# Compressed-attention values with their high, low and high parts stacked in 96 rows, one matmul per head in place of three

## The chip, the cores and the metric

The kernel runs on one core of a Trainium2 chip. The metric is the device time of one execution in microseconds (us), lower is better. Matmul operands are float32 numbers split in two `fp32r` parts, a high part (what the conversion keeps) and a low part (what it loses), so that a product needs three matmuls: high by high, high by low, low by high. The helper `mm3` issues these three, on lines 171, 172 and 173.

## The reference

One layer of a decoder trunk on 512 tokens of width 2048: RMS norm, an input projection, eight forgetting-attention heads (FoX) and eight NSA query heads in two key/value groups, an output projection, and a SwiGLU feed-forward part of width 5632. An NSA head adds three branches, each with a sigmoid gate. The change touches the compressed branch alone, in which 31 compressed keys and values per group stand for the 512 tokens:

```python
k_cmp = _rms_norm(_compress(kc.reshape(B, T, G, Dh), cmp_pos_k, cmp_w_k), cmp_k_norm)
v_cmp = _compress(vc.reshape(B, T, G, Dh), cmp_pos_v, cmp_w_v)
...
s_c = jnp.einsum("bqgrd,bngd->bgrqn", qn_b, k_cmp).astype(f32) * scale
s_c = s_c - slopes[None, :, :, None, None] * dist_c
p_c = _masked_softmax(s_c, dist_c >= 0)
o_c = jnp.einsum("bgrqn,bngd->bqgrd", p_c.astype(dt), v_cmp)
...
o_nsa = g_b[..., 0:1] * o_c + g_b[..., 1:2] * o_s + g_b[..., 2:3] * o_w
```

## The kernel before

The core works through stages: a first pass over the sixteen k tiles of the input (`x`), which makes the first projections (`ps_first`, lines 651 to 683) and the row sum of squares (`acc`, then `fr_r1` and `ps_r1`, lines 259 and 260); the remaining projections, woven by `weave` with the attention heads; the output projection; and the feed-forward part, which begins at about 750 us of the span.

In the attention stage the generator `nsa(h)` is the side work and the projections of coming heads are the main work; `weave` hands out steps of both. Instructions then go through a scheduler of the programming layer, which may reorder them on each engine by its own estimates, except where `pin` keeps them. Each engine executes its own queue in order.

The compressed values of both groups are made once in `compress("vc")`: 32 matmuls accumulate `z`, its parts `zs` are multiplied by `rows` (a matrix of ones that adds a row of `z` to the positional term), and the result `zr`, 64 rows (32 for each group), is split by `split` into `Vc[:, 0]` (high, a ScalarE copy, line 82) and `Vc[:, 1]` (low, a VectorE subtraction, line 79). Keys (`"kc"`) go through the same lines.

`compressed(h, q, o)` makes a head in three steps. First the scores, softmax and gate; the probabilities go to columns `gs` of a 64-column tile `pc[g]`, whose other 32 columns stay zero from a memset on line 286. Then four transposes (line 539) put the probabilities of the four token blocks into a PSUM tile of 64 rows, `pcT`, of the tag "t" (two buffers), and `split2` makes the two parts `ptc`. Last, `mm3` adds the product with `Vc` to the head's output `o`:

```python
mm3(o, Vc[:, 0], Vc[:, 1], *pt, False, True)
```

All 64 rows take part; the zero columns of `pc[g]` cancel the other group. This is the last product of the head, after the selected branch (`pt_s`) and the window branch (`pt_w`); `keep` then copies `o` (line 449).

Of the kernel before, what the change touches and what calls it, by code (L numbers as in the profile page):

```python
# [9 lines left out]
F32 = mybir.dt.float32  # L10
FR = mybir.dt.float32r
AF = mybir.ActivationFunctionType
OP = mybir.AluOpType
# [4 lines left out]
P = 128  # L18
D = 2048
T = 512  # L20
# [3 lines left out]
NB = T // P  # L24
# [46 lines left out]
def hybrid_layer(ctx: ExitStack, tc: tile.TileContext, xT, vec, ffb, wfg, wfirst, win, cmpw, wout, wgu, wdn, out):  # L71
    nc = tc.nc
# [5 lines left out]
    def tt(*args, op):  # L78
        return pin(nc.vector.tensor_tensor(*args, op=op))  # L79

    def act(*args, **kw):
        return pin(nc.scalar.activation(*args, **kw))  # L82
# [10 lines left out]
    ap_ = att.enter_context(tc.tile_pool(name="att", bufs=1))  # L93
    ps = ctx.enter_context(tc.tile_pool(name="ps", bufs=1, space=PSUM))
# [6 lines left out]
    def big(i):  # L101
        at = i * 2 * T + OFF_BIG[i]
        return bigm[:, at:at + 2 * T].rearrange("p (s t) -> p s t", s=2)
# [23 lines left out]
    def ftile(name):  # L127
        return pers.tile([P, T], F32, tag="f", name=name, bufs=4)

    def split(dst, src, scale=None, neg=None):  # L130

        if scale is None:
            h = act(dst[:, 0], src, AF.Copy)
            tt(dst[:, 1], src, dst[:, 0].bitcast(F32), op=OP.subtract)
            return h
        else:
            nc.scalar.activation(dst[:, 0], src, AF.Copy, scale=scale)
            nc.vector.scalar_tensor_tensor(dst[:, 1], src, scale, dst[:, 0].bitcast(F32),
                                           op0=OP.mult, op1=OP.subtract)
# [4 lines left out]
    def split2(dst, src, scale=None):  # L144

        if scale is None:
            h = act(dst[0], src, AF.Copy)
            tt(dst[1], src, dst[0].bitcast(F32), op=OP.subtract)
        else:
            h = act(dst[0], src, AF.Copy, scale=scale)  # L150
            nc.vector.scalar_tensor_tensor(dst[1], src, scale, dst[0].bitcast(F32), op0=OP.mult, op1=OP.subtract)
        return h
# [17 lines left out]
    def mm3(o, lh, ll, rh, rl, start, stop):  # L170
        nc.tensor.matmul(o, lh, rh, start=start, stop=False)  # L171
        nc.tensor.matmul(o, lh, rl, start=False, stop=False)  # L172
        nc.tensor.matmul(o, ll, rh, start=False, stop=stop)  # L173
# [60 lines left out]
    def v1(i):  # L234
        return vt[:, i:i + 1]

    ident = pers.tile([P, P], F32, name="ident")
# [42 lines left out]
    mc = ap_.tile([P, NB, 32], F32, name="mc")  # L280
    nc.vector.tensor_scalar(mc, dc, 0.0, None, op0=OP.is_ge)
    nc.gpsimd.affine_select(dc, dc, pattern=[[P, NB], [-16, 32]], compare_op=OP.is_ge, fill=FAR, base=-31, channel_multiplier=1)
    pc = []
    for g in range(2):
        t = ap_.tile([P, NB, 64], F32, name=f"pc{g}")
        nc.vector.memset(t, 0.0)
        pc.append(t)

    gains = ap_.tile([P, 6], F32, name="gains")
    nc.vector.tensor_scalar_mul(gains, vt[:, 0:6], -0.5 / HD)  # L290
# [8 lines left out]
    nc.vector.tensor_tensor(rowsf, ident[:, :64], ident[:, 64:], op=OP.add)  # L299
    rows = ap_.tile([P, 64], FR, name="rows")  # L300
    nc.vector.tensor_tensor(rows, rowsf, rowsf[:, 31:32].to_broadcast([P, 64]), op=OP.add)
    rcol = ap_.tile([P, NB], F32, name="rcol")


# [22 lines left out]
    def loose(name, shape=(P, T)):  # L327
        return oxp.tile(list(shape), FR, tag="ox", name=name, bufs=16)
# [148 lines left out]
    def compress(which):  # L477

        z = ps.tile([P, T], F32, tag="s", name=f"z_{which}", bufs=2)[:, :2 * P].rearrange("p (a c) -> p a c", a=2)
        wi = 0 if which == "kc" else 4  # L480
        for b in range(8):
            st = oxp.tile([P, T], F32, tag="ox", name=f"ws_{which}{b}", bufs=16)
            nc.sync.dma_start(st, cmpw[wi + b // 2, :, b % 2 * T:(b % 2 + 1) * T])
            wp = ap_.tile([P, 2, T], FR, tag="kv", name=f"wp_{which}{b}", bufs=5)
            split(wp, st)
            for jj in range(4):
                l = 4 * b + jj
                ws = slice(jj * P, (jj + 1) * P)
                nc.tensor.matmul(z, live[which, l // 16][:, l % 16 * P:(l % 16 + 1) * P], wp[:, :, ws],
                                 start=(l == 0), stop=(l == 31))  # L490
                if l % 2:
                    yield

        zs = ap_.tile([P, 2, 2 * P], FR, tag="nb", name=f"zs_{which}", bufs=2)
        split(zs, z.rearrange("p a c -> p (a c)"))
        yield
        r = ps.tile([P, T], F32, tag="t", name=f"zr_{which}", bufs=2)[:64, :P]
        for hl in range(2):
            nc.tensor.matmul(r, rows, zs[:, hl, :P], start=(hl == 0), stop=False)
            nc.tensor.matmul(r, rows[:64], zs[:64, hl, P:], start=False, stop=(hl == 1))  # L500
        if which == "kc":
            zks = ftile("zks")[:64, :P]
            ss = ap_.tile([64, 4], F32, name="ss")
            nc.scalar.activation(zks, r, AF.Square, accum_out=ss[:, 0:1])
            rsqrt(ss[:, 1:2], ss[:, 0:1], float(HD), ss[:, 2:3])
            nc.vector.tensor_scalar_mul(zks, r, ss[:, 1:2])
            yield
            zkT = ps.tile([P, 64], F32, tag="t", name="zkT", bufs=2)
            nc.tensor.transpose(zkT, zks, ident[:64, :64])
            split(Kc, zkT, v1(V_CK))  # L510
        else:
            split(Vc, r)

    def compressed(h, q, o):
        g = h // 4
        slope = 2.0 ** -(h + 1)
        s = ps.tile([P, NB, 64], F32, tag="m", name=f"sc{h}")
        gs = slice(32 * g, 32 * g + 32)
        for i in range(NB):
            qs = slice(i * P, (i + 1) * P)  # L520
            nc.tensor.matmul(s[:, i, :], q[0][:, qs], Kc[:, :, gs], start=True, stop=False)
            nc.tensor.matmul(s[:, i, 32:64], q[1][:, qs], Kc[:, 0, gs], start=False, stop=True)
        t = ap_.tile([P, NB, 32], F32, tag="ct", name=f"ct{h}", bufs=2)
        st = ap_.tile([P, 3, NB], F32, tag="st", name=f"stc{h}", bufs=4)
        nc.vector.scalar_tensor_tensor(t, dc, slope, s[:, :, 0:32], op0=OP.mult, op1=OP.add)
        nc.vector.tensor_tensor(t, t, s[:, :, 32:64], op=OP.add)
        nc.vector.tensor_reduce(st[:, 0], t, axis=AX.X, op=OP.min)
        nc.vector.tensor_tensor(t, t, st[:, 0, :, None].to_broadcast([P, NB, 32]), op=OP.subtract)
        nc.scalar.activation(t, t, AF.Exp, scale=-1.0)
        nc.vector.tensor_tensor(t, t, mc, op=OP.mult)  # L530
        nc.vector.tensor_reduce(st[:, 1], t, axis=AX.X, op=OP.add)
        nc.vector.tensor_scalar_max(st[:, 2], st[:, 1], 1e-30)
        nc.vector.reciprocal(st[:, 2], st[:, 2])
        nc.vector.tensor_tensor(st[:, 2], st[:, 2], gate[:, :, 3 * h], op=OP.mult)
        nc.vector.tensor_tensor(pc[g][:, :, gs], t, st[:, 2, :, None].to_broadcast([P, NB, 32]), op=OP.mult)
        yield
        b = ps.tile([P, T], F32, tag="t", name=f"pcT{h}", bufs=2)
        for i in range(NB):
            nc.tensor.transpose(b[:64, i * P:(i + 1) * P], pc[g][:, i, :], ident)
        pt = [loose(f"ptc{h}{p}")[:64] for p in range(2)]  # L540
        split2(pt, b[:64])
        yield
        mm3(o, Vc[:, 0], Vc[:, 1], *pt, False, True)
        yield

    qq = ap_.tile([P, 2, 2, T], FR, name="qq")
# [1 line left out]
    cumd = dr.tile([NH, T], F32, name="cumd")  # L548
    ncq = ap_.tile([P, NB, NH], F32, name="ncq")
    Kc = ap_.tile([P, 2, 64], FR, name="Kc")  # L550
    Vc = ap_.tile([64, 2, P], FR, name="Vc")
    tokens = {}

    def gates():
# [101 lines left out]
    for k in range(NK):  # L656
# [4 lines left out]
        t = big(k)  # L661
# [10 lines left out]
        for j in range(4):  # L672
            c = slice(j * P, (j + 1) * P)
            mm3(first[j], wp[:, 0, c], wp[:, 1, c], t[:, 0], t[:, 1], k == 0, k == NK - 1)
        for hl in range(2):
            nc.tensor.matmul(first[4][:64], wf[:, k], t[:, hl], start=(k == 0 and hl == 0),
                             stop=(k == NK - 1 and hl == 1))
# [73 lines left out]
    for i, h in enumerate(order[:-1]):  # L751
        t = big(i)
# [3 lines left out]
    t = big(NK - 1)  # L756
# [48 lines left out]
    for m in range(NK):  # L805
        n = m // 2 + HALF * (m % 2)
# [231 lines left out]
    for j in range(NJ):  # L1038
        for which in range(2):
            q = [ps.tile([P, T], F32, tag=tag, name=f"q{which}{j}_{i}", bufs=BUFS[tag])  # L1040
                 for i, tag in enumerate(SETS[which])]
            for g in range(NG):
                i = (2 * j + which) * NG + g
# [15 lines left out]
                for wp in range(2):  # L1059
                    for kk in range(2):  # L1060
# [3 lines left out]
                        for fa, fb, b, h in PROD:  # L1064
                            o = q[b][:, h * 256:(h + 1) * 256]
                            for xp in range(2 - wp):
                                nc.tensor.matmul(o, w[wp][:, fb, cs], a[:, xp, fa],  # L1067
                                                 start=(k == 0 and h == 0 and wp == 0 and xp == 0),
                                                 stop=(g == NG - 1 and kk == 1 and wp == 1), skip_group_check=True)
# [24 lines left out]
    def banks(name, tags):  # L1094
        return [ps.tile([P, T], F32, tag=tag, name=f"{name}_{i}", bufs=BUFS[tag]) for i, tag in enumerate(tags)]
# [67 lines left out]
    for ps_ in range(4):  # L1163
        p, second = ps_ // 2, ps_ % 2
        b = [banks(f"pd{ps_}{i}", t) for i, t in enumerate(TAGS)]
# [151 lines left out]
```

## Time and profile before

| what | value |
|---|---|
| median of 3 runs | 2114.24 us (2113.95 to 2114.7) |
| profiled execution, its own time | 2114.38 us |
| its span in the trace | 2112.6 us |
| NSA heads' compressed products in the trace | 153 to 403 us of the span |
| feed-forward part | from about 750 us |

Times in the trace count from the start of the span. PE is TensorE, PEld its weight loads, DVE is VectorE, ACT is ScalarE, POOL is GpSimd. A timeline row gives the start, the duration, the engine, the line, the operation with output and inputs, the shape of the part of the array that a matmul or weight load uses (128\*128 is the whole array; the first number is rows), and the tile's shape. Durations of matmuls overlap, since they are pipelined; what one costs in a full queue is read from the distance of two starts. A text in brackets says how long the engine idled before the instruction and what ended the idle time.

### The profile page before, as it was taken

The numbers are of one execution on the slowest core, as the hardware profiler recorded it, in microseconds if no ns is written. First come the engines' busy times: TensorE is split into PE (matmuls) and PEld (weight loads), VectorE is DVE, ScalarE is ACT, GpSimd is POOL, SyncE is SP. The second block draws the span as 40 slices with busy tenths as digits, with TensorE's granted clock in tenths as the row PEclk, the third lists the DMA queues.
The fourth block names the chain that finished last, engine by engine and source line by source line (L and its number), as shares of the span: only waits on it lengthen the run. The fifth ranks groups of instructions, "written<-read, shape, count | busy, mean of one in ns | idle before, by whom it ended". The sixth has DMA issues, their size and how long they took to land.

```text
span 2112.6 us, 37997 instructions
## 1 busy us (share of the span) xinstructions
PE 2101.6 (99%) x15675; PEld 1974.6 (93%) x15675; DVE 1675.4 (79%) x2458; ACT 999.7 (47%) x1242; POOL 190.7 (9%) x283
## 2 busy tenths in 40 slices
PE   9999999999999999999999999999999999999999
PEld 7878988888988888999999999999999999999999
DVE  6667667554567454999999999899999987889898
ACT  5555555444455343544334343343343455565554
POOL 0000000111211000111111111111111000000000
PEclk9999999999999999999999999999999999999999
DMA  5422111222222444676776777777787798579865
GB/s 196 160 75 62 61 58 58 65 86 85 90 85 75 152 137 137 170 188 202 193 195 189 193 197 182 201 187 184 205 191 195 225 335 270 151 233 329 302 174 149
DMA packets 113486, 349.63 MB, mean 165 GB/s; under 512 B 13592, under 2 KB 13592, under 8 KB 113312
## 3 DMA queue, kind: packets, MB, share of 16 engines
q1 hardware_dynamic: 85552, 270.33, 39.5%
q0 software_dynamic: 22144, 52.44, 14.0%
q10 hardware_dynamic: 5616, 24.43, 2.9%
q8 instruction: 122, 2.00, 0.4%
q14 instruction: 52, 0.43, 0.1%
HBM read 318.56 MB, written 74.73 MB: 186 GB/s over the span
## 4 chain that ended last, share of the span: by engine, by line
PE 85%; issue 9%; DVE 3%; POOL 1%; ACT 1%; DMA 0%; POOLq 0%; SPq 0%; ACTq 0%; DVEq 0%
PE q L1067 39%; PE pd L1206 13%; PE pd L1211 6%; PE po L172 3%; PE po L173 3%; PE po L171 3%; PE ps_vs L369 2%; PE ps_vf L369 1%; PE ps_qn L171 1%; PE ps_qn L173 1%; PE ps_qn L172 1%; POOL nbf L628 1%; PE ps_first L171 1%; PE ps_first L173 1%; PE ps_first L172 1%
## 5 line engine op out<-in xcount | busy, mean ns | idle before, releaser
L82 ACT ACTIVATE bigm<-r 128x1792 fp32r<-128x1792 f32 x174 | 298.2, 1714 | 461.1 <-PE q L1067 263.4
L79 DVE TENSOR_TENSOR bigm<-r,bigm 128x1792 fp32r<-128x1792 f32 x174 | 351.5, 2020 | 13.2 <-ACT bigm L82 12.7
L79 DVE TENSOR_TENSOR r<-r 128x512 f32<-128x512 f32 x522 | 267.2, 512 | 27.5 <-DMA r<-wgu 15.2
L1067 PE MATMUL q<-bigm 128*128 128x256 f32 x1848 | 217.5, 276 | 0.2 <-ACT bigm L82 0.2
L1067 PE MATMUL q<-formy,bigm 128*128 128x256 f32 x1848 | 217.1, 276 | 0.0
L1067 PE MATMUL q<-forma,bigm 128*128 128x256 f32 x1848 | 216.8, 276 | 0.0
L1067 PE MATMUL q<-formx,bigm 128*128 128x256 f32 x1848 | 216.8, 276 | 0.0
L1067 PEld LDWEIGHTS q<-bigm 128*128 128x128 f32 x1848 | 213.3, 188 | 0.6 <-ACT bigm L82 0.4
L1067 PEld LDWEIGHTS q<-formy,bigm 128*128 128x128 f32 x1848 | 213.1, 188 | 0.1
L1067 PEld LDWEIGHTS q<-forma,bigm 128*128 128x128 f32 x1848 | 213.0, 188 | 0.1
L1067 PEld LDWEIGHTS q<-formx,bigm 128*128 128x128 f32 x1848 | 212.9, 188 | 0.0
L124 POOL DMA_DIRECT2D wsum<-wdn x176 | 119.8, 687 | 878.7 <-ACT bigm L82 773.7
L1206 PE MATMUL pd<-bigm 128*128 128x256 f32 x1200 | 146.9, 276 | 0.0
L1206 PEld LDWEIGHTS pd<-bigm 128*128 128x128 f32 x1200 | 141.0, 188 | 0.0
L79 DVE TENSOR_TENSOR bigm<-wd,bigm 128x1024 fp32r<-128x1024 f32 (+1 forms) x62 | 107.8, 1739 | 12.3 <-ACT bigm L82 12.2
L82 ACT ACTIVATE bigm<-rawm 128x768 fp32r<-128x768 f32 (+2 forms) x72 | 66.0, 927 | 98.2 <-PE pd L1211 63.8
L369 PE MATMUL ps_vf<-wp_vf,bigm 128*128 128x256 f32 x768 | 101.7, 282 | 0.0
L171 PE MATMUL po<-bigm,wp_o 128*128 128x512 f32 x256 | 99.7, 389 | 0.0
L172 PE MATMUL po<-bigm,wp_o 128*128 128x512 f32 x256 | 99.7, 389 | 0.0
L173 PE MATMUL po<-bigm,wp_o 128*128 128x512 f32 x256 | 99.6, 389 | 0.0
L369 PEld LDWEIGHTS ps_vf<-wp_vf,bigm 128*128 128x128 f32 x768 | 95.1, 189 | 1.5 <-issue 0.7
L82 ACT ACTIVATE bigm<-wd 128x1024 fp32r<-128x1024 f32 (+1 forms) x62 | 91.1, 1469 | 10.7 <-DVE wd L79 6.1
(479 smaller groups left out, 3975.8 us busy)
## 6 DMA issues: line engine op xcount, KB each, us to landing
r<-wgu SPq DMA_DIRECT2D x174, 512.0 KB, 4.3
wsum<-wdn POOLq DMA_DIRECT2D x176, 256.0 KB, 5.1
rawm<-ad SPq DMA_DIRECT2D x44, 512.0 KB, 6.9
wd<-wdn SPq DMA_DIRECT2D x40, 512.0 KB, 6.0
wd<-wsum SPq DMA_DIRECT2D x40, 512.0 KB, 7.0
ad<-cb ACTq DMA_DIRECT2D x22, 896.0 KB, 6.0
rawm<-ad SPq DMA_DIRECT2D x44, 384.0 KB, 3.8
ws_o<-wout SPq DMA_DIRECT2D x28, 512.0 KB, 3.6
```

Of the source, the lines that this page charges most:

```text
L79: return pin(nc.vector.tensor_tensor(*args, op=op))
L82: return pin(nc.scalar.activation(*args, **kw))
L124: d = nc.gpsimd.dma_start(step[0], step[1], **step[2])
L171: nc.tensor.matmul(o, lh, rh, start=start, stop=False)
L172: nc.tensor.matmul(o, lh, rl, start=False, stop=False)
L173: nc.tensor.matmul(o, ll, rh, start=False, stop=stop)
L369: nc.tensor.matmul(z[b][:, t * 2 * HD:(t + 1) * 2 * HD], x[:, xp, at], wp[w][:, ws], start=(c == 0 and kk == 0 and t == 0 and n == 0), sto ...
L628: nc.gpsimd.tensor_scalar(nb[:, :n], ck[:, :n], ncq[:, i, h:h + 1], 1.0, op0=OP.add, op1=OP.mult)
L1067: nc.tensor.matmul(o, w[wp][:, fb, cs], a[:, xp, fa], start=(k == 0 and h == 0 and wp == 0 and xp == 0), stop=(g == NG - 1 and kk == 1 and ...
L1206: nc.tensor.matmul(b[q][k][:, h * 256:(h + 1) * 256], w[0][:, fb, q * P:(q + 1) * P], a[xp][:, fa], start=(j == 0 and h == 0 and xp == 0), ...
L1211: nc.tensor.matmul(b[q][k][:, h * 256:(h + 1) * 256], w[1][:, fb, q * P:(q + 1) * P], a[0][:, fa], start=False, stop=(j == NJ - 1), skip_g ...
```

## The change

Three parts are stacked in the 96 contraction rows of one matmul: values high, low, high against probabilities high, high, low. The rows of only the head's own group are used, so 3 times 32 rows suffice.

- `rows3` is `rows` with each group's 32 columns repeated three times (three VectorE copies at the start). For the values `compress("vc")` multiplies `zs` by `rows3` of each group: eight matmuls instead of four, into 96 rows.
- `Vc` becomes a list of two tiles of 96 rows; each is one copy by ScalarE and one VectorE subtraction on rows 32 to 63.
- `pc` becomes one 96-column tile per head, written by one VectorE multiplication that repeats the probabilities three times; the two memsets go.
- The four transposes give 96 rows; one ScalarE copy makes all high parts and one VectorE subtraction turns rows 64 to 95 into low parts.
- One matmul per head takes the place of `mm3`.

```diff
-    pc = []
-    for g in range(2):
-        t = ap_.tile([P, NB, 64], F32, name=f"pc{g}")
-        nc.vector.memset(t, 0.0)
-        pc.append(t)
...
+    rows3 = ap_.tile([P, 2, 3, 32], FR, name="rows3")
+    for n in range(3):
+        nc.vector.tensor_copy(rows3[:, :, n], rows.bitcast(F32).rearrange("p (g c) -> p g c", g=2))
...
-        r = ps.tile([P, T], F32, tag="t", name=f"zr_{which}", bufs=2)[:64, :P]
-        for hl in range(2):
-            nc.tensor.matmul(r, rows, zs[:, hl, :P], start=(hl == 0), stop=False)
-            nc.tensor.matmul(r, rows[:64], zs[:64, hl, P:], start=False, stop=(hl == 1))
+        r = ps.tile([P, T], F32, tag="t", name=f"zr_{which}", bufs=2)
+        r, by = ([r[:64, :P]], [rows]) if which == "kc" else (
+            [r[:96, g * P:(g + 1) * P] for g in range(2)], [rows3[:, g].rearrange("p n c -> p (n c)") for g in range(2)])
+        for n, (o, m) in enumerate(zip(r, by)):
+            for hl in range(2):
+                nc.tensor.matmul(o, m, zs[:, hl, :P], start=(n == 0 and hl == 0), stop=False, skip_group_check=True)
+                nc.tensor.matmul(o, m[:64], zs[:64, hl, P:], start=False, stop=(hl == 1), skip_group_check=True)
...
-            split(Vc, r)
+            for o, v in zip(r, Vc):
+                nc.scalar.activation(v, o, AF.Copy)
+                nc.vector.tensor_tensor(v[32:64], o[32:64], v[32:64].bitcast(F32), op=OP.subtract)
...
-        nc.vector.tensor_tensor(pc[g][:, :, gs], t, st[:, 2, :, None].to_broadcast([P, NB, 32]), op=OP.mult)
+        pc = ap_.tile([P, NB, 96], F32, name="pc")
+        nc.vector.tensor_tensor(pc.rearrange("p i (n c) -> p n i c", n=3), t[:, None].to_broadcast([P, 3, NB, 32]),
+                                st[:, 2, None, :, None].to_broadcast([P, 3, NB, 32]), op=OP.mult)
         yield
         b = ps.tile([P, T], F32, tag="t", name=f"pcT{h}", bufs=2)
         for i in range(NB):
-            nc.tensor.transpose(b[:64, i * P:(i + 1) * P], pc[g][:, i, :], ident)
-        pt = [loose(f"ptc{h}{p}")[:64] for p in range(2)]
-        split2(pt, b[:64])
-        yield
-        mm3(o, Vc[:, 0], Vc[:, 1], *pt, False, True)
+            nc.tensor.transpose(b[:96, i * P:(i + 1) * P], pc[:, i, :], ident)
+        pt = loose(f"ptc{h}")
+        nc.scalar.activation(pt[:96], b[:96], AF.Copy)
+        nc.vector.tensor_tensor(pt[64:96], b[64:96], pt[64:96].bitcast(F32), op=OP.subtract)
+        yield
+        nc.tensor.matmul(o, Vc[g], pt[:96], start=False, stop=True)
         yield
...
-    Vc = ap_.tile([64, 2, P], FR, name="Vc")
+    Vc = [ap_.tile([96, P], FR, name=f"Vc{g}") for g in range(2)]
```

More of the change, by code (lines that the diff above doesn't have):

```diff
@@ L503, in compress @@
             ss = ap_.tile([64, 4], F32, name="ss")
-            nc.scalar.activation(zks, r, AF.Square, accum_out=ss[:, 0:1])
+            nc.scalar.activation(zks, r[0], AF.Square, accum_out=ss[:, 0:1])
             rsqrt(ss[:, 1:2], ss[:, 0:1], float(HD), ss[:, 2:3])
-            nc.vector.tensor_scalar_mul(zks, r, ss[:, 1:2])
+            nc.vector.tensor_scalar_mul(zks, r[0], ss[:, 1:2])
             yield
```

## The prediction

> **What bounds the kernel now.** I read the page first, for the engine that is never free; then the stretches around the change, to see whether this holds there; then the timeline of TensorE at the product that is changed.
>
> ```profile
> PE 2101.6 (99%) x15675; PEld 1974.6 (93%) x15675; DVE 1675.4 (79%) x2458; ACT 999.7 (47%) x1242; POOL 190.7 (9%) x283
> PE 85%; issue 9%; DVE 3%; POOL 1%; ACT 1%; DMA 0%; POOLq 0%; SPq 0%; ACTq 0%; DVEq 0%
> ```
>
> TensorE is busy for 99% of the span, and the chain that ended last runs over it for 85%. Busy does not mean well used, since pipelined matmuls overlap in their durations: a microsecond is won where starts lie closer together or a start goes away.
>
> ```profile
> core 0: us, PE busy (x) PEld busy (x) DVE busy (x) ACT busy (x) POOL busy (x), PEclk, DMA share, GB/s
> 345.00:403.00 58.00, 57.40 (x395) 51.91 (x394) 39.13 (x111) 29.58 (x67) 3.58 (x4) 1.00 0.18 56
> ```
>
> In this stretch of the attention stage, the last two NSA heads, TensorE idles for 0.60 of 58 us, VectorE works 39.13 us (67%), DMA is at 0.18, and the granted clock is 1.00. So VectorE, ScalarE and DMA have room, and what TensorE loses or gains there is lost or gained by the kernel; later stages take their weights as TensorE consumes them, so they only start earlier.
>
> **The product of a head.** This is the last product of head 0, with the matmuls around it:
>
> ```profile
> 175.35 0.39 PE L173 MATMUL ps_qn<-bigm,wp_qn 128*128 128x512 f32 x1
> 175.67 0.49 PE L171 MATMUL on<-ptc,Vc 64*128 64x512 f32 x1
> 176.00 0.39 PE L172 MATMUL on<-ptc,Vc 64*128 64x512 f32 x1
> 176.23 0.39 PE L173 MATMUL on<-ptc,Vc 64*128 64x512 f32 x1
> 176.56 0.50 PE L171 MATMUL ps_kw<-bigm,wp_kw 128*128 128x512 f32 x1
> 176.90 0.39 PE L172 MATMUL ps_kw<-bigm,wp_kw 128*128 128x512 f32 x1
> ```
>
> ```profile
> 175.67 0.18 PEld L171 LDWEIGHTS on<-ptc,Vc 64*128 64x128 f32 x1 [0.36 <-issue]
> ```
>
> Two matmuls of 512 columns in the same array shape start 0.23 us apart (176.00 to 176.23). Where the shape goes from 128\*128 to 64\*128 the distances are 0.32 and 0.33, and on the way back 0.33 and 0.34; the weight load starts together with its matmul after 0.36 us of "issue". From 175.35 to 176.90 lie five starts in 1.55 us; at 0.23 they would take 1.15. So the two changes of shape cost 0.40 us per head.
>
> ```profile
> L171 PE MATMUL on<-ptc,Vc x8: 492/493/493, 175.7 to 401.7; 64*128 64x512 f32 x8
> ```
>
> The same lengthened first matmul (492 to 493 ns against 0.39 us of the others) stands in all eight heads, so head 0 speaks for all.
>
> In the changed program as built, the one matmul per head carries the shape 128\*128, as 96 rows are more than 64. Then no change of shape is left, and of the five starts two are gone: 3 x 0.23 = 0.69 us. That saves 1.55 - 0.69 = 0.86 us per head, of which 2 x 0.23 = 0.46 is matmuls and 0.40 is shape; 8 x 0.86 = **6.9 us less**. If the shape change stayed, it would be 8 x 0.46 = 3.7.
>
> **The transposes** go from 64 to 96 columns, and from the shape 128\*64 to 128\*128. I compare four of `pcT` with four of `pT_w`, which have the full shape already:
>
> ```profile
> 274.68 0.40 PE L173 MATMUL ps_qn<-bigm,wp_qn 128*128 128x512 f32 x1
> 274.92 0.60 PE L539 MATMUL pcT<-ident,pc 128*64 128x128 f32 x4
> ...
> 275.58 0.39 PE L172 MATMUL ps_qn<-bigm,wp_qn 128*128 128x512 f32 x1
> ```
>
> ```profile
> 163.76 0.39 PE L173 MATMUL ps_qn<-bigm,wp_qn 128*128 128x512 f32 x1
> 163.99 0.60 PE L423 MATMUL pT_w<-ident,p_w 128*128 128x128 f32 x4
> ...
> 164.66 0.39 PE L172 MATMUL ps_qn<-bigm,wp_qn 128*128 128x512 f32 x1
> ```
>
> From the matmul ahead to the second behind it is 0.90 us in both. I take 0 for this edit. The Trainium skill, page TensorEngine Tiling (Array Packing), section Key Properties, says that changing the tiling mode, and not just the tile, drains TensorE; 128x64 is one of the configurations that the page lists. By that sentence the transposes would pay for two changes per head now and the edit would take them away; the trace shows such a price where the number of rows changes and none where only columns do. I go by the rows here, and keep the other as a rival.
>
> **`compress("vc")`** issues four matmuls more, two pairs of a full-height and a 64-row one. The nearest rows are the same pairs of the keys:
>
> ```profile
> 106.29 0.22 PE L499 MATMUL zr_kc<-zs_kc,rows 128*64 128x128 f32 x1
> 106.44 0.27 PE L500 MATMUL zr_kc<-zs_kc,rows 64*64 64x128 f32 x1
> 106.64 0.28 PE L499 MATMUL zr_kc<-zs_kc,rows 128*64 128x128 f32 x1
> 106.85 0.27 PE L500 MATMUL zr_kc<-zs_kc,rows 64*64 64x128 f32 x1
> 107.05 0.51 PE L171 MATMUL ps_kw<-bigm,wp_kw 128*128 128x512 f32 x1
> ```
>
> A pair takes 0.35 (106.29 to 106.64) to 0.41 us (106.64 to 107.05). In the changed order the two new pairs follow the last old one directly, as the second pair here follows the first, so I take 0.41: **0.8 us more**, once, between 0.7 and 0.8. The extra copy and subtraction for `Vc` (both of 128 columns) run on ScalarE and VectorE beside TensorE: 0.
>
> **`rows3`** adds three VectorE copies of 128x64 in the first pass, where VectorE is not idle:
>
> ```profile
> 10.43 0.22 DVE L301 TENSOR_TENSOR rows<-rowsf 128x64 fp32r<-128x64 f32 x1
> 10.57 1.48 DVE L683 TENSOR_TENSOR acc<-acc,sq 128x512 f32<-128x512 f32 x2
> 11.97 0.75 DVE L138 SCALAR_TENSOR_TENSOR bigm<-x,vt,bigm 128x512 fp32r<-128x512 f32 x1
> 12.63 0.68 DVE L683 TENSOR_TENSOR acc<-acc,sq 128x512 f32<-128x512 f32 x1
> 13.23 0.75 DVE L138 SCALAR_TENSOR_TENSOR bigm<-x,vt,bigm 128x512 fp32r<-128x512 f32 x1
> 13.89 0.69 DVE L79 TENSOR_TENSOR w0p<-w,w0p 128x512 fp32r<-128x512 f32 x1
> ```
>
> ```profile
> 14.63 0.30 PEld L173 LDWEIGHTS ps_first<-bigm,w0p 128*128 128x128 f32 x2 [0.21 <-DVE w0p L79]
> 1.26 0.43 DVE L242 CAST ones<-onesf 128x128 fp32r<-128x128 f32 x1
> ```
>
> Each row starts before the one ahead has ended, without a gap, and TensorE waits for the low part of `w0p` that ends this run. The copies stand behind the first `acc`, so their time reaches TensorE in full. From below: the 128x64 `rows` takes 0.14 us to the next start, so 3 x 0.14 = 0.4. From above: 3 x 0.43 of the largest such cast (twice the columns) = 1.3. A gain is excluded, since work is only added here; the two memsets that go stood before 2 us, ahead of the first data. I take **0.5 us more**, nearest to the row of the same size.
>
> The scheduler also moves the first matmul of the row sum (`ps_r`) over a hundred matmuls forward in TensorE's queue, to just behind five `wf` matmuls:
>
> ```profile
> 31.58 0.63 ACT L82 ACTIVATE fr_r<-acc 128x512 fp32r<-128x512 f32 x1 [1.03 <-DVE acc L683]
> 31.95 1.31 PE L676 MATMUL ps_first<-bigm,wf 128*64 128x512 f32 x5
> ```
>
> Its input is there at 32.21, and TensorE gets to it at about 31.95 + 5 x 0.23 = 33.10. Everything behind it in the queue would wait with it, but 0.9 us are left, and the copies delay both sides alike: 0.
>
> **The probabilities.** `pc` is written with 384 elements per partition instead of 128.
>
> ```profile
> L539 PE MATMUL pcT<-ident,pc x32: 270/272/301, 168.3 to 397.7; 128*64 128x128 f32 x32
> L535 DVE TENSOR_TENSOR pc<-ct,stc x8: 280/292/294, 163.8 to 391.2; 128x128 f32<-128x128 f32 x8
> ```
>
> ```profile
> 159.96 0.41 DVE L79 TENSOR_TENSOR pt_s<-pT_s,pt_s 128x256 fp32r<-128x256 f32 x1
> ```
>
> From 0.29 us at 128 elements and 0.41 at 256, 384 take about 0.53: 0.24 more per head. In the first head the transposes start 4.5 us after `pc`, in the last about 6; that covers it. Without cover it would be 8 x 0.24 = 1.9 us. `pc` has a single buffer, but eight heads lie between 168.3 and 397.7, some 33 us apart, so its transposes have long ended.
>
> ```profile
> 209.17 0.68 DVE L79 TENSOR_TENSOR ptc<-pcT,ptc 64x512 fp32r<-64x512 f32 x1
> ```
>
> ```profile
> 211.41 0.49 PE L171 MATMUL on<-ptc,Vc 64*128 64x512 f32 x1
> ```
>
> The one matmul now waits for the low part as well, which before only the second did. In head 1 that part ends at 209.85, 1.56 us ahead of the start. Queued behind the matmul are the next projections, so a late part would stop TensorE; with 0.24 us added it is not late. In the last two heads the scheduler reorders a few steps of VectorE and TensorE; of the 0.60 us of idle time there some may go or as much may come: 0, plus or minus 0.6.
>
> **Sum.** -6.9 + 0.8 + 0.5 = -5.6 us. From the profiled execution's 2114.38 us (1.8 more than its span of 2112.6) this gives 2108.8; the median of the runs lies 0.14 lower, so **2108.6 us**. With the bounds (0.7 to 0.8, 0.4 to 1.3, plus or minus 0.6) the forecast itself lies between 2107.8 and 2110.0.
>
> **The rivals.** A measurement of this kernel can tell about 0.2% from no change, 4.2 us: below 2110.0 is faster, above 2118.5 slower.
>
> *Shape change stays.* If 96 rows are loaded like a partial array, the 0.40 us per head stay: -3.7 + 0.8 + 0.5 = -2.4, 2111.8 us, no change that can be told. For it: the row above shows the price for 64 rows, and no row has 96. Against it: the built program's 128\*128. Chance 0.10.
>
> *Column changes cost too.* If the transposes pay the 0.40 us per head that the row changes pay, 3.2 us more go: 2105.4 us. That is the skill's sentence above taken at its word. Against it stand the two equal 0.90 us. Chance 0.04.
>
> *The low part comes late (slower).* The one matmul has its place behind VectorE's subtraction. It decides from 1.56 us of delay in head 1; were VectorE 3 us late in every head with that slack, TensorE would stand 1.44 us eight times, 11.5 us, and 2108.6 would become 2120.1. For it: VectorE runs 0.53 us per head in one go where it ran 0.29. Against it: 0.24 is far from 1.56, and VectorE is at 67%. Chance 0.04.
>
> **How the numbers follow.** The forecast has 0.82, the rivals 0.10, 0.04 and 0.04. Of the forecast's 0.82 about 0.04 falls above 2110.0. Faster: 0.78 + 0.04 = 0.82. Same: 0.10 + 0.04 = 0.14. Slower: 0.04. The range takes in the forecast's bounds with a microsecond below for gaps that close behind the earlier matmuls, and reaches up to the first rival: 2106.8 to 2112.0.
>
> **What would show it.** In the changed profile: matmuls `on<-ptc` with shape 128\*128, eight of them, the start behind each 0.23 us later and no "issue" ahead; transposes still 0.90 us from matmul to matmul; three copies after 10.5 us and a wait of about 0.7 us on `w0p` at 15 us; two new pairs near 143 us. It would be wrong if `on<-ptc` idled on VectorE, or if 0.32 us starts were left around it.

## The result, and the profile after

| | before | after |
|---|---|---|
| median of 20 runs each, us | 2114.48 (2113.74 to 2115.24) | 2109.94 (2109.4 to 2145.72) |
| ratio, 95% interval | | 0.998 (0.9974 to 0.9986) |
| profiled execution, us | 2114.38 | 2109.57 |
| its span, us | 2112.6 | 2107.9 |

The change makes the kernel faster by 4.5 us, 0.2%; 2108.6 us (-5.6 from the trace) was predicted. The median lies within the stated range of 2106.8 to 2112.0 us, and only 0.06 us below the 2110.0 that the prediction set as the bound of faster. Two slow executions of about 2145 us make the upper end of the runs after and are left out of the ratio; the trace of `e2_one64`, used below, is of such an execution, with the extra time (35.9 us) behind the last product.

The page after, its busy times and the shares of the chain that ended last:

```profile
PE 2096.4 (99%) x15663; PEld 1972.8 (94%) x15663; DVE 1677.6 (80%) x2460; ACT 999.8 (47%) x1243; POOL 190.8 (9%) x283
PE 84%; issue 9%; DVE 3%; ACT 1%; POOL 1%; DMA 0%; POOLq 0%; SPq 0%; ACTq 0%; DVEq 0%
```

The kernel is as bound by TensorE as it was. TensorE's count of matmuls falls by 12: 16 products less, 4 matmuls of `compress("vc")` more. The stretches, with the same columns as before:

```profile
345.00:403.00 58.00, 57.38 (x399) 52.41 (x398) 39.90 (x110) 30.52 (x68) 3.58 (x4) 1.00 0.14 46
```

TensorE still idles for only 0.62 of 58 us and the granted clock is 1.00; it gets through 399 records there where it got through 395. VectorE has 39.90 us for 39.13.

**The product.** TensorE's timeline after, around the product of head 0, and the eight products in one row (duration as minimum/median/maximum in ns, then first and last start):

```profile
176.20 0.39 PE L173 MATMUL ps_qn<-bigm,wp_qn 128*128 128x512 f32 x1
176.43 0.40 PE L552 MATMUL on<-ptc,Vc 96*128 96x512 f32 x1
176.67 0.40 PE L171 MATMUL ps_kw<-bigm,wp_kw 128*128 128x512 f32 x1
176.90 0.40 PE L172 MATMUL ps_kw<-bigm,wp_kw 128*128 128x512 f32 x1
```

```profile
L552 PE MATMUL on<-ptc,Vc x8: 393/395/397, 176.4 to 398.1; 96*128 96x512 f32 x8
```

From the projection matmul ahead to the second one behind, 1.55 us has become 0.70 (176.20 to 176.90). Every start is 0.23 or 0.24 us from the last, and the median product takes 395 ns where the first of three took 493. The profile writes the shape as 96\*128, not 128\*128, and it costs nothing all the same.

**A ledger by segments.** Between one head's product and the next both kernels issue the same matmuls (180, 228, 221, 165, 148, 180 and 212 records for heads 1 to 7), in the same order but for a few ahead of heads 5, 6 and 7. So each segment of the trace can be set beside the other's by its starts: a *product* from the matmul ahead of it to the second behind it, an *interval* from there to the matmul ahead of the next product. This is the one for head 5, whose ends stand in these rows, of before and then of after:

```profile
315.12 0.39 PE L172 MATMUL ps_qn<-bigm,wp_qn 128*128 128x512 f32 x1
...
342.20 0.28 PE L173 MATMUL on<-pt_w,vs 128*128 128x256 f32 x1
```

```profile
311.96 0.40 PE L172 MATMUL ps_qn<-bigm,wp_qn 128*128 128x512 f32 x1
...
339.84 0.29 PE L173 MATMUL on<-pt_w,vs 128*128 128x256 f32 x1
```

It took 27.08 us before and takes 27.88 after: 0.8 us of what the product saves is given back there. The whole ledger, each kernel less before, in us (segments of several kernels that are told of below stand beside it; the times up to 141 us are counted from the span's start):

| segment | after | `e1_shape` | `e3_pc128` | `e4_zrfull` | `h1_nonorm` |
|---|---|---|---|---|---|
| up to the first row sum of `vc` (141 us) | -0.12 | +0.20 | +0.81 | -0.36 | -0.13 |
| row sums of `vc` | +0.98 | +0.01 | +0.99 | -0.16 | +0.98 |
| eight products | -6.75 | -3.07 | -6.78 | -6.76 | -6.76 |
| interval ahead of head 4's product | +0.25 | +0.08 | +0.03 | +0.27 | +0.54 |
| of head 5's | +0.79 | +0.25 | +0.80 | +0.79 | -0.03 |
| of head 7's | +0.57 | +0.42 | +0.56 | +0.54 | +0.21 |
| intervals of heads 0, 1, 2, 3, 6 | -0.05 | +0.03 | +0.06 | +0.28 | 0.00 |
| up to the feed-forward part | +0.08 | +0.12 | +0.04 | -0.27 | +0.01 |
| feed-forward part | -0.50 | +0.61 | -0.03 | -0.17 | -0.06 |
| sum (to 0.01) | -4.76 | -1.36 | -3.52 | -5.84 | -5.24 |

The feed-forward part is the same code in all of them, and moves from -0.50 to +0.61 between one trace and the next: that much is the difference between executions, so the ledger is good to a tenth or two within the attention stage and not over the whole span. The same holds for the first row.

**Where 1.6 us goes.** The list of TensorE's waits between 300 and 345 us (in total, times, longest) is empty before and has two rows after; the timelines of TensorE and of VectorE show the reason of the first:

```profile
PE s_s L171 <- DVE st_s L399: 0.3, 1, 0.3
PE pT_s L422 <- DVE pt_s L79: 0.2, 1, 0.2
```

```profile
314.15 0.33 PE L173 MATMUL s_s<-ks,qq 128*128 128x384 f32 x1
314.84 0.39 PE L171 MATMUL s_s<-ks,qq 128*128 128x256 f32 x1 [0.35 <-DVE st_s L399]
```

```profile
311.97 0.69 DVE L249 SCALAR_TENSOR_TENSOR tmp_kf<-ss_kf,tmp_kf 128x512 f32<-128x512 f32 x1
312.69 0.69 DVE L254 SCALAR_TENSOR_TENSOR y_kf<-tmp_kf,y_kf 128x512 f32<-128x512 f32 x1
313.42 0.75 DVE L341 SCALAR_TENSOR_TENSOR t_kf<-t_kf,gains,y_kf 128x512 f32<-128x512 f32 x1
314.09 0.68 DVE L399 CUSTOM_DVE_ANT_0 p_s<-s_s,nb 128x512 f32<-128x512 f32 x1
```

The scores `s_s` of an NSA head go to PSUM tiles of the tag "s", which has two buffers: the third tile (256 columns) has to wait until VectorE has read the first. VectorE stands in the normalization of the first FoX key (three instructions, 312.0 to 314.1 us) until then. Before, TensorE was about 1 us later relative to this normalization (from before to after its first instruction moved by 2.19 us, from 314.16 to 311.97, and the last matmul of the second tile by 3.18, from 317.33 to 314.15), and it was VectorE that waited:

```profile
314.16 0.69 DVE L249 SCALAR_TENSOR_TENSOR tmp_kf<-ss_kf,tmp_kf 128x512 f32<-128x512 f32 x1
...
316.59 0.69 DVE L400 CUSTOM_DVE_ANT_0 p_s<-s_s,nb 128x512 f32<-128x512 f32 x1 [0.23 <-PE s_s L173]
317.21 0.08 DVE L400 DVE_READ_ACCUMULATOR2_ANT st_s<- 128x1 f32 x1
```

```profile
317.51 0.28 PE L171 MATMUL s_s<-ks,qq 128*128 128x256 f32 x1
```

So after the change TensorE arrives early at a buffer that VectorE has not read, and part of the gain turns into a wait. The start of the third tile lies 0.69 us behind the one ahead of it, where it lay 0.18 behind before, and the start behind it takes 0.22 us for 0.12: some 0.6 us of the interval's 0.8 are lost at this place. 0.2 more are the wait of `pT_s`, further down the same head.

Ahead of head 7's product the list of waits (345 to 405 us) shows nothing of the kind, but the rows do. TensorE's timeline after, and VectorE's:

```profile
373.92 0.39 PE L171 MATMUL s_s<-ks,qq 128*128 128x256 f32 x1
...
376.01 0.50 PE L171 MATMUL s_w<-kw,qq 128*128 128x512 f32 x1
```

```profile
373.18 0.68 DVE L399 CUSTOM_DVE_ANT_0 p_s<-s_s,nb 128x512 f32<-128x512 f32 x1
373.78 0.08 DVE L399 DVE_READ_ACCUMULATOR2_ANT st_s<- 128x1 f32 x1
```

VectorE has read the first tile at 373.86, and the third starts at 373.92. The first tile of the window branch (`s_w`, the same tag) starts at 376.01, 0.05 us after VectorE has read the third. Against the usual distances each of the two places loses 0.32 us (0.21 ahead of the start and 0.11 behind it), and neither did before, when VectorE had read the first tile 0.37 us ahead of the third one's start. The wait of `pT_s` in the same head is 0.1 us shorter than before. So this is the same kind of wait. That is read from these rows alone; no run of the kernel after takes it away. The experiments test the place ahead of head 5.

### The profile page after: what moved, and what is told of

It is laid out like the page before. It is cut to its first block, busy times and chain, and to the rows that moved or that the text cites. A ratio compares the mean times of both kernels' runs of the same rounds, so it can differ in the third digit from the quotient of the medians.

```text
span 2107.9 us, 37975 instructions
## 1 busy us (share of the span) xinstructions
PE 2096.4 (99%) x15663; PEld 1972.8 (94%) x15663; DVE 1677.6 (80%) x2460; ACT 999.8 (47%) x1243; POOL 190.8 (9%) x283
## 4 chain that ended last, share of the span: by engine, by line
PE 84%; issue 9%; DVE 3%; ACT 1%; POOL 1%; DMA 0%; POOLq 0%; SPq 0%; ACTq 0%; DVEq 0%
PE q L1076 39%; PE pd L1215 13%; PE pd L1220 7%; PE po L173 3%; PE po L172 3%; PE po L171 3%; PE ps_vs L368 2%; PE ps_vf L368 1%; PE ps_qn L171 1%; PE ps_qn L173 1%; PE ps_qn L172 1%; POOL nbf L637 1%; PE ps_first L171 1%; PE ps_first L173 1%; PE ps_first L172 1%
```

## The experiments

Each time is set against runs of before on the same chip.

### The shape alone: `e1_shape`

The kernel before, still with three products, but padded with zero rows from 64 to 96. (A GpSimd copy, not shown, puts the zeros into `Vc`.)

```diff
-        t = ap_.tile([P, NB, 64], F32, name=f"pc{g}")
+        t = ap_.tile([P, NB, 96], F32, name=f"pc{g}")
...
-            nc.tensor.transpose(b[:64, i * P:(i + 1) * P], pc[g][:, i, :], ident)
+            nc.tensor.transpose(b[:96, i * P:(i + 1) * P], pc[g][:, i, :], ident)
...
-    Vc = ap_.tile([64, 2, P], FR, name="Vc")
+    Vc = ap_.tile([96, 2, P], FR, name="Vc")
```

> The kernel before with its three matmuls per head kept, but padded with zero rows from 64 to 96, so that they use the full array shape; nothing else changes. If the change of array shape costs 0.40 us per head, the time falls by up to 3.2 us, to 2111.3 us, less what TensorE then waits for VectorE; the distances around the product are all 0.23 us. If only the number of matmuls counts, the time stays at 2114.5 us.

Measured: 2112.46 us against 2114.71, ratio 0.9987 (0.9979 to 0.9996). Its timeline at head 0:

```profile
175.57 0.39 PE L173 MATMUL ps_qn<-bigm,wp_qn 128*128 128x512 f32 x1
175.80 0.39 PE L171 MATMUL on<-ptc,Vc 96*128 96x512 f32 x1
...
176.50 0.39 PE L171 MATMUL ps_kw<-bigm,wp_kw 128*128 128x512 f32 x1
176.73 0.40 PE L172 MATMUL ps_kw<-bigm,wp_kw 128*128 128x512 f32 x1
```

Five starts in 1.16 us for 1.55: the change of shape costs 0.39 us at a 64-row product and none at a 96-row one, with as many matmuls. Eight of them make 3.07 us, and 0.75 of it is given back in the same three intervals as in the kernel after. The transposes got wider here too and nothing fell in their places, which is one more sign that they had paid nothing.

### One product of 64 rows: `e2_one64`

The kernel after with two stacked parts, not three; it leaves out the product with the values' low part.

```diff
-        nc.tensor.matmul(o, Vc[g], pt[:96], start=False, stop=True)
+        nc.tensor.matmul(o, Vc[g], pt[:64], start=False, stop=True)
```

> The changed kernel with 64 instead of 96 rows in its one matmul; it leaves out the product of the values' low part. If the shape change has a price of its own, the product gains only the two matmuls, 8 x 0.46 = 3.7 us, the value compression still costs 1.0, and little is given back: about 2112 us, with a product of 1.09 us from matmul to matmul instead of 0.69. If it is the number of matmuls that counts, the time is that of the changed kernel, 2109.9 us.

Measured: 2112.8 us against 2114.71, ratio 0.9992 (0.9973 to 1.0011). The interval of the ratio is too wide to say more than "about as before", but the timeline at head 0 is plain:

```profile
178.12 0.39 PE L173 MATMUL ps_qn<-bigm,wp_qn 128*128 128x512 f32 x1
178.44 0.49 PE L551 MATMUL on<-ptc,Vc 64*128 64x512 f32 x1
178.86 0.50 PE L171 MATMUL ps_kw<-bigm,wp_kw 128*128 128x512 f32 x1
179.19 0.39 PE L172 MATMUL ps_kw<-bigm,wp_kw 128*128 128x512 f32 x1
```

1.07 us: the two matmuls have gone (0.48 less than 1.55) and the price of the shape stays. All eight products give 0.46 or 0.47 us. With `e1_shape` the saving of 0.85 us divides into 0.39 for the shape and 0.46 for two matmuls.

### The longer write of `pc`: `e3_pc128` and `f2_pool`

`e3_pc128` is the kernel after, with the probabilities written once (128 elements a partition, not 384); the other 64 columns stay zero, so that it leaves out two of the three products.

```diff
-        nc.vector.tensor_tensor(pc.rearrange("p i (n c) -> p n i c", n=3), t[:, None].to_broadcast([P, 3, NB, 32]),
-                                st[:, 2, None, :, None].to_broadcast([P, 3, NB, 32]), op=OP.mult)
+        nc.vector.tensor_tensor(pc[:, :, :32], t, st[:, 2, :, None].to_broadcast([P, NB, 32]), op=OP.mult)
```

> The changed kernel with the probabilities written once, into 32 of the 96 columns, the others zero from the start; it leaves out two of the three products. VectorE's write is then as long as before (0.29 us). If the 1.6 us that are given back between the products come from this longer write, they go, and the time is about 2108.3 us. If they come from TensorE reaching the next head's scores earlier than VectorE can take them, they stay, and the time stays at 2109.9 us with the wait before the scores of head 5.

Measured: 2110.24 us against 2114.71, ratio 0.9979 (0.997 to 0.9989). The 0.25 us ahead of head 4 go, the 0.80 and 0.56 ahead of heads 5 and 7 stay.

`f2_pool` moves the whole write to GpSimd.

```diff
-        nc.vector.tensor_tensor(pc.rearrange("p i (n c) -> p n i c", n=3), ...
+        nc.gpsimd.tensor_tensor(pc.rearrange("p i (n c) -> p n i c", n=3), ...
```

> The changed kernel with the threefold write of the probabilities on GpSimd instead of VectorE. If that write is behind the 0.25 us that head 4 gives back, those go, 2109.7 us, and the waits of heads 5 and 7 stay. If GpSimd is too slow for the transposes (over 4.5 us), TensorE waits for it and the time rises above 2110.

Measured: 2110.21 us against 2114.8, ratio 0.998 (0.9971 to 0.9989). The intervals of heads 4, 5 and 7 give back 0.11, 0.79 and 0.63. Both runs say that the longer write costs some 0.2 us in one head, and isn't what takes the rest.

### Row sums at full height: `e4_zrfull`

The 64-row matmuls of the row sums become full ones, by a second matrix of ones whose lower half is zero.

```diff
-                nc.tensor.matmul(o, m[:64], zs[:64, hl, P:], start=False, stop=(hl == 1), skip_group_check=True)
+                nc.tensor.matmul(o, half, zs[:, hl, P:], start=False, stop=(hl == 1), skip_group_check=True)
```

> The changed kernel with all matmuls of the compressed keys' and values' row sums at full height: the half-height ones use a second matrix of ones whose lower 64 rows are zero. If the change of shape is what a pair costs (0.35 to 0.41 us), the eight matmuls of the values fall from about 1.7 to about 0.7 us and the four of the keys by about 0.5: about 1.3 us less than the changed kernel, 2108.6 us. If a short matmul costs that much by itself, the time stays at 2109.9 us.

Measured: 2108.85 us against 2114.71, ratio 0.998 (0.997 to 0.999), 1.1 us below the median of after. Of its eight executions three took 2113 to 2115 us, and the ratios of the two kernels can't be told apart; what shows the gain is the trace. TensorE's timeline of the two added pairs and the start behind them, in the kernel after and then in this one:

```profile
143.31 0.30 PE L501 MATMUL zr_vc<-zs_vc,rows 128*96 128x128 f32 x1
143.55 0.30 PE L502 MATMUL zr_vc<-zs_vc,rows 64*96 64x128 f32 x1
143.77 0.30 PE L501 MATMUL zr_vc<-zs_vc,rows 128*96 128x128 f32 x1
144.01 0.30 PE L502 MATMUL zr_vc<-zs_vc,rows 64*96 64x128 f32 x1
144.24 0.44 PE L171 MATMUL s_s<-ks,qq 128*128 128x384 f32 x1
```

```profile
142.56 0.25 PE L508 MATMUL zr_vc<-zs_vc,rows_vc 128*96 128x128 f32 x1
142.65 0.25 PE L509 MATMUL zr_vc<-zs_vc,rows_vc 128*96 128x128 f32 x1
...
142.90 0.39 PE L171 MATMUL s_s<-ks,qq 128*128 128x384 f32 x1
```

A pair that goes from 128 to 64 rows and back takes 0.46 us (143.31 to 143.77); the same pair at one height 0.17 (142.56 to 142.90 for two). So 0.29 of the 0.46 is the change of shape. The row sums cost 0.98 us more than before in the kernel after and 0.16 less here.

### Side work later: `f1_later`, `f4_before_later`, `f3_all`

In the last two NSA stages `weave` starts the side work, the NSA heads, after four steps of the main work, not two. `f1_later` has this on the kernel after, `f4_before_later` on the kernel before.

```diff
-    weave(stagger(kf(0), nsa_q(6), nsa_q(7)), chain(nsa(4), nsa(5)), 3 * N - 2, 2 * NS, 2)
-    weave(stagger(qf(0), vf(0)), chain(nsa(6), nsa(7)), 3 * NK, 2 * NS, 2)
+    weave(stagger(kf(0), nsa_q(6), nsa_q(7)), chain(nsa(4), nsa(5)), 3 * N - 2, 2 * NS, 4)
+    weave(stagger(qf(0), vf(0)), chain(nsa(6), nsa(7)), 3 * NK, 2 * NS, 4)
```

> The changed kernel with the NSA heads 4 to 7 woven in one projection step later (the delay of the last two weaves 4 instead of 2), so that the scores of heads 5 and 7 stand some 0.7 us later in TensorE's queue against the norms that VectorE works on. If TensorE comes too early for VectorE there, the 0.79 us ahead of head 5's product and the 0.57 us ahead of head 7's mostly go, 2108.7 us. If they have another cause, the time stays at 2109.9 us.

> The kernel before with the same later weave of heads 4 to 7. In it TensorE does not wait for the scores of head 5, so if the later weave only takes away that wait, nothing is won here: 2114.5 us within 0.3. If the later weave is better by itself, it gains as much as in the changed kernel, about 2113.3.

Measured: `f1_later` 2109.91 us against 2114.8, ratio 0.9981 (0.9972 to 0.999), no gain over after; `f4_before_later` 2115.25, ratio 1.0001 (0.9993 to 1.001). As a repair it fails, since the order itself costs a few tenths. As a control it tells more. With this order in both, the change is worth 5.3 us between the medians where it is worth 4.5 in the old one; the intervals of the ratios are too wide to tell these apart, but the traces agree. In them the intervals of heads 4 to 7 take 1.01, -0.48, +0.75 and -0.35 us with the change, and 0.97, -0.48, +0.57 and -0.73 without (each less before; some matmuls move from one interval to the next). The change gives back 0.04, 0.00, 0.18 and 0.38, 0.6 in all for 1.6, and nothing at head 5; at head 7 a wait of 0.3 us for the buffer of the scores has come. What is given back depends on where the two queues meet, and is not a fixed price of the change.

`f3_all` puts `e4_zrfull` and the later side work together, with the transposes of `rstd` at full height.

```diff
-            nc.tensor.transpose(tr[:, i, :], rstd[:NH, i * P:(i + 1) * P], ident[:NH, :NH])
+            nc.tensor.transpose(tr[:, i, :], rstd[:, i * P:(i + 1) * P], ident)
```

> The changed kernel with the full-height row sums, the later weave of heads 4 to 7, and the four transposes of the row scale (8 rows high before) at full height. If the parts add, 1.1 us for the row sums, up to 1.2 for the weave and about 0.4 for two changes of shape around the transposes: 2107.2 us. If the weave does nothing, 2108.4.

Measured: 2108.43 us against 2114.8, ratio 0.9975 (0.9966 to 0.9984). This is the time expected for a weave that does nothing. By its interval it can't be told from `e4_zrfull`.

### The normalization on GpSimd: `g1_norm`, `g2_before_norm`, `g3_best`

For the first FoX key and query the last norm steps leave VectorE. `g1_norm` is the kernel after with this, `g2_before_norm` the kernel before, `g3_best` has it on `e4_zrfull`.

```diff
-        rsqrt(y, o, float(HD), ftile(f"tmp_{name}"), False)
-        nc.vector.scalar_tensor_tensor(t, t, gain, y, op0=OP.mult, op1=OP.mult)
+        if name in ("kf0", "qf0"):
...
+            nc.vector.scalar_tensor_tensor(tmp, o, HD * EPS, tmp, op0=OP.add, op1=OP.mult)
+            nc.gpsimd.tensor_scalar(tmp, tmp, -3.0 * HD, gain, op0=OP.add, op1=OP.mult)
+            nc.gpsimd.tensor_tensor(y, tmp, y, op=OP.mult)
+            nc.gpsimd.tensor_tensor(t, t, y, op=OP.mult)
```

> The changed kernel with the last steps of the norms of the first FoX key and query (two VectorE instructions of 0.7 us each) done on GpSimd, in TensorE's unchanged order. If TensorE waits ahead of heads 5 and 7 because VectorE is busy with these norms, the 0.79 and 0.57 us there shrink to 0.2 and less, 1.0 us in all, 2108.9 us, and the wait for the scores of head 5 is gone. If the two losses have another cause, they stay and the time with them, 2109.9 us.

> The kernel before with the same norms on GpSimd. TensorE hardly waits for VectorE there, so the time stays at 2114.5 us, within 0.3. If it falls by a microsecond too, the norms cost in both kernels and are no part of what the change gives back.

> The changed kernel with the full-height row sums and the norms on GpSimd together. If both parts add, 1.1 + 1.0 us less than the changed kernel: 2107.8 us.

Measured: `g1_norm` 2114.36 us against 2114.63, ratio 0.9999 (0.999 to 1.0008), 4.4 above the kernel after; `g2_before_norm` 2118.89, ratio 1.0022 (1.0013 to 1.0031); `g3_best` 2112.91, ratio 0.9994 (0.9985 to 1.0003). All three miss. From `g1_norm`: one of the two slow multiplications on GpSimd, VectorE behind it, and TensorE behind that:

```profile
315.10 1.29 POOL L348 TENSOR_TENSOR t_kf<-t_kf,y_kf 128x512 f32<-128x512 f32 x1
```

```profile
317.09 0.69 DVE L79 TENSOR_TENSOR kf<-t_kf,kf 128x512 fp32r<-128x512 f32 x1 [2.78 <-ACT kf L82]
317.70 0.55 DVE L409 CUSTOM_DVE_ANT_0 p_s<-s_s,nb 128x384 f32<-128x384 f32 x1
```

```profile
318.31 0.33 PE L171 MATMUL s_s<-ks,qq 128*128 128x128 f32 x1 [2.12 <-DVE st_s L409]
```

The wait at the 256-column tile is gone, as the theory has it. But the low part of the key, which VectorE makes, stands in VectorE's queue ahead of the next `p_s` and now waits for GpSimd (through ScalarE's copy of the high part), and TensorE waits 2.12 us for the buffer one tile later. So the place is what the theory says, a late normalization in front of `p_s` reaches TensorE through this buffer, and the repair made it later. That holds without the change too: the intervals of heads 5 and 7 grow by 1.81 and 1.49 us in `g2_before_norm`.

### Without the normalization: `h1_nonorm`

The kernel after, leaving out VectorE's part of the normalization of the first FoX key and query.

```diff
+        if name not in ("kf0", "qf0"):
             rsqrt(y, o, float(HD), ftile(f"tmp_{name}"), False)
             nc.vector.scalar_tensor_tensor(t, t, gain, y, op0=OP.mult, op1=OP.mult)
+        else:
+            nc.scalar.activation(y, o, AF.Ln, scale=1.0 / HD, bias=EPS)
+            nc.scalar.activation(y, y, AF.Exp, scale=-0.5)
+            nc.scalar.activation(ftile(f"tmp_{name}"), y, AF.Square)
```

> The kernel after, leaving out the normalization of the first FoX key and the first FoX query (its last three VectorE instructions, 0.69 + 0.69 + 0.75 us for each), so that VectorE comes to the scores of the next NSA head about 2 us earlier; the order of TensorE's queue differs only in where some projection matmuls stand. Theory (the time that TensorE wins in the product is given back in heads 5 and 7 because TensorE comes to the next head's scores while VectorE is still in this normalization, and their buffer is not yet read): the 0.79 and 0.57 us given back ahead of the products of heads 5 and 7 fall to 0.2 or less each, the wait of s_s on st_s near 315 us is gone, and the time is about 2108.9 us. Rival (the time is given back by the new order of TensorE's queue itself, or by TensorE's work that has to be done in these heads anyway): the two segments stay within 0.2 us of 0.79 and 0.57, and the time is that of the kernel after, 2109.9 us.

Measured: 2109.62 us against 2114.56, ratio 0.9976 (0.9966 to 0.9985). VectorE and TensorE at the same scores:

```profile
313.74 0.69 DVE L404 CUSTOM_DVE_ANT_0 p_s<-s_s,nb 128x512 f32<-128x512 f32 x1 [1.51 <-PE s_s L173]
```

```profile
314.45 0.34 PE L173 MATMUL s_s<-ks,qq 128*128 128x384 f32 x1
314.63 0.28 PE L171 MATMUL s_s<-ks,qq 128*128 128x256 f32 x1
```

VectorE waits for TensorE again, and the third tile of scores follows the second at once (0.18 us, for 0.69 in the kernel after). The interval of head 5 gives back nothing (-0.03 for +0.79), with the matmuls in the order of before. That settles what took head 5's.

The interval of head 7 gives back 0.21 (for +0.57; expected 0.2 or less), but not because this wait has gone. TensorE's timeline there:

```profile
372.83 0.39 PE L171 MATMUL s_s<-ks,qq 128*128 128x256 f32 x1 [0.16 <-DVE st_s L404]
```

The third tile still waits for VectorE, which stands in a 1.23 us split of a weight until 372.05 and reads the first tile only then; it loses 0.43 us, and `s_w` 0.28 more. What has gone is a wait of `pT_s` that the kernel before has too (0.30 us at 388.58, some 0.6 us in its starts), and TensorE's order differs there. So at head 7 VectorE's lateness is shown, and the normalization as its cause is not.

The time doesn't follow as far: the interval of head 4 gives back 0.29 more than in the kernel after, with a wait of 0.3 us of `pT_w` on `pt_w` in a VectorE queue that has also been reordered. The median of the undisturbed executions is 2109.34 us, 0.5 below that of the kernel after (2109.88) and not the 1 us expected, less than the intervals of the ratios can tell.

## Why the prediction was right, point by point

- **TensorE alone sets the end: right in the main.** Each gain and each loss in the table is a distance of TensorE's starts, and reaches the end. But at three places VectorE set those starts, and 1.6 us were lost to it (last term below).
- **The products, -6.9: right**, -6.75. The division into 0.46 for matmuls and 0.40 for the shape is measured as 0.46 and 0.39. The reason given (96 rows carry the shape 128\*128) was right in effect and wrong in name, as the profile says 96\*128; so the rival of a shape price that stays is refuted by the distances and not by the label.
- **Transposes, 0: right.** TensorE's timeline after, to be set against the two rows of before that are 0.90 us apart:

```profile
272.97 0.39 PE L173 MATMUL ps_qn<-bigm,wp_qn 128*128 128x512 f32 x1
273.20 0.60 PE L547 MATMUL pcT<-ident,pc 128*96 128x128 f32 x4
...
273.88 0.39 PE L172 MATMUL ps_qn<-bigm,wp_qn 128*128 128x512 f32 x1
```

0.91 us. The Trainium skill, TensorEngine Tiling (Array Packing), Key Properties, says that changing the tiling mode drains TensorE. The runs agree where the number of rows changes (0.39 us there and back around 64 rows, `e1_shape`) and do not show it where only columns do, nor at 96 rows.

- **`compress("vc")`, +0.8: too low by 0.2**, +0.98. The pair was taken from the keys at 0.41 us; with 96 columns the two new ones take 0.46 and 0.47 (143.31 to 144.24), and the two old ones 0.03 more each. `e4_zrfull` shows that 0.29 of a pair's 0.46 is the change of shape.
- **`rows3`, +0.5: the step that over-counted.** VectorE's and the weight loads' timelines after:

```profile
11.22 0.54 DVE L300 CAST rows<-rows 128x64 fp32r<-128x64 f32 x3
14.20 0.68 DVE L79 TENSOR_TENSOR w0p<-w,w0p 128x512 fp32r<-128x512 f32 x1
```

```profile
14.93 0.30 PEld L173 LDWEIGHTS ps_first<-bigm,w0p 128*128 128x128 f32 x2 [0.25 <-DVE w0p L79]
```

The copies did push the low part of `w0p` back, from 13.89 to 14.20, and the waiting load from 14.63 to 14.93. But the load's wait grew only from 0.21 to 0.25 us, where 0.7 was forecast, since the scheduler had put one more `w0p` matmul ahead of it. And the wait of a load was not one of the matmuls: before, its first matmul starts at 14.69, 0.23 us behind the one ahead, as in a full queue. TensorE's 300th matmul, at 71 us, stands 0.05 us later than before. "Their time reaches TensorE in full" was wrong: VectorE's delay is filled with a matmul that had to be done anyway.
- **The longer `pc`, hidden: nearly.** It takes 0.56 us where 0.53 was forecast, and costs 0.2 us in head 4 alone (`e3_pc128`).
- **The low part of the one product, hidden: right.** No product waits on VectorE.
- **Reorders in the last heads, 0 plus or minus 0.6: the mis-sized term.** Three intervals of the attention stage, not only the last heads', give back 1.6 us. The rows of before allow the sum, and it wasn't made. VectorE waits 0.23 us for `s_s` at 316.59, and has read the first tile at 317.29, 0.22 us before TensorE asks for its buffer at 317.51. So TensorE can come 0.45 us earlier there and not more; of the 0.84 us that the product of head 4 gives, 0.39 turn into a wait. The trace after loses 0.51 between the starts there, since the normalization had also come 0.12 us later against TensorE (it moved by 2.19 us, and the matmul ahead of head 4's product by 2.31, from 313.57 to 311.26). VectorE's 67% was read as room at this place, and there it had 0.45 us.

The two misses, 0.5 too much for `rows3` and 1.6 too little for the waits, with 0.2 for `compress("vc")` and 0.1 for the products, make 1.4; a feed-forward part that was 0.5 shorter by chance brought the traces to -4.76. That the sum came out no further off is partly luck: the two wrong terms have opposite signs, and 0.5 us of one hid as much of the other.

What stays open: whether the normalization is what makes VectorE late at head 7, and why VectorE's queue costs head 4 0.29 us more in `h1_nonorm`. A third buffer for the scores, which would test the wait without touching VectorE, was not tried.

## What to carry to other kernels

Where a bound engine is made faster, look in its consumers' rows for places where they wait for it: that wait, with the slack of the buffers behind it, was about all the gain that could pass here (0.45 us), at a consumer that was busy for 67%. Look at the neighbours of a small matmul and not only at its own duration: a 64-row matmul among full-height ones cost 0.39 us beside its 0.23, and padding with zero rows took that away. Work that leaves a queue must also come back in time for what stands behind it there; here a move to a slower engine that feeds the old one only lengthened the wait.

## What the runs showed of the hardware

- The price of an array shape depended on the rows: 64 among 128 cost 0.39 us there and back with 512 columns (1.55 us for five starts, 1.16 when padded), 96 among 128 nothing (starts 0.23 to 0.24 us apart), 96 or 64 columns among 128 nothing that shows (0.91 and 0.90 us around four transposes).
- A multiplication of two 128x512 tiles took 1.29 us on GpSimd, and a VectorE instruction of that size 0.69, a ratio of 1.9. The Trainium skill, GPSIMD Engine Reference, section 3.1, has a `tensor_tensor` add as 1.96 times slower there; the trace agrees, and the expectation of `g1_norm` should have started from it.
- Executions of the same first pass can start differently. In the kernel after, the warm-up matmuls (`ps_warm`, 512 columns) stand 0.43 us apart until 5.5 us, and from 7 us the first products 0.23. In the profile of `f3_all` they stand 0.43 us apart until 10 us, at a granted clock of 1.00:

```profile
8.46 0.63 PE L173 MATMUL ps_first<-bigm,w0p 128*128 128x512 f32 x1
8.89 0.63 PE L172 MATMUL ps_first<-bigm,w0p 128*128 128x512 f32 x1
```

`e2_one64` and `g2_before_norm` start so too. It is worth 1.75 us up to 141 us (`f3_all` is 1.39 behind before there, `e4_zrfull` with the same first pass 0.36 ahead), over a third of this change. The Trainium skill, TensorE: Matmul & The Clock Gate, Part 1, says that the array starts at half rate, and that its warm-up depends on the phase of a free-running window at the kernel's start; the distance agrees with its 426.7 ns for cold matmuls of 512 columns, and the granted clock in the profile doesn't show it.
